# Sparse/differential attention trunk: layer 0's first projections in two contraction halves, half of its conditioning rows on TensorE

## The chip, the cores and the metric

One NeuronCore of one Trainium2 chip runs the whole program. The metric is the device time of one execution in microseconds, from the first to the last instruction and the little that lies around them. Half of a per cent is about 12 us here.

## What is computed

A decoder trunk of two layers on 256 tokens with 2048 features, in fp32. Each layer is a token mixer and a squared-ReLU MLP, and each of these four parts is conditioned by shift, scale and gate vectors that come from one vector `c`:

```python
mod_all = jnp.einsum('bd,lde->lbe', jax.nn.silu(c), ada_w) + ada_b[:, None, :]
for i in range(DEPTH):
    sh1, sc1, g1, sh2, sc2, g2 = jnp.split(mod_all[i][:, None, :], 6, axis=-1)
    h = rms_norm(x, attn_norm_g[i]) * (1.0 + sc1) + sh1
    y = nsa_mixer(h, ...) if i % 2 == 0 else diff_mixer(h, ...)
    x = x + g1 * y
    h = rms_norm(x, mlp_norm_g[i]) * (1.0 + sc2) + sh2
    x = x + g2 * sqrelu_mlp(h, mlp_w1[i], mlp_w2[i])
```

The mixer of layer 0 projects `h` to 16 query heads (`q`), and to `kc, vc, ks, vs, kw, vw` (512 columns each) and 48 gates. `kc` and `vc` are compressed: 32 tokens at a time plus a position term, through a matrix of 4096 by 256, SiLU, and a matrix of 256 by 128. Each query head then has three branches (compressed, selected, window) with their own softmax, mixed by the gates. Layer 1's mixer is differential attention.

## The kernel before

Features lie on the 128 partitions in 16 tiles (`kt`), tokens in the free dimension. Weights are read once, in pieces of 128x1024 (`load`, 512 KB each, pool of 5). Most products are made of three fp32r matmuls: `split` writes a rounded copy `wH` on ScalarE and the rest `wL` on VectorE, and `xs_mm` or `ws_mm` multiply high by high, high by low and low by high. A few products use plain fp32 matmuls without a split; each of these appears in the trace as two MATMUL records.

A conditioning element is the dot product of one row of 2048 numbers with silu(c); 128 of them (one kt of one vector) are one `ada` row, a DMA of 1 MB and one VectorE instruction with an accumulator (line 163, for the first two vectors line 170). There are 12 vectors of 16 rows. The first two are read in the opening loop; the other 160 stand in the list `ada_q`, and `ada_step(rate)` takes rows from it as the matmul loops go on: at RA, RB, RC rows per step in the first mixer. Their buffer pool has three (`adap`), and the instruction has lowered priority. The tile framework orders each engine's instructions by priority and readiness before the run; on the chip each engine and each DMA queue then runs in that order.

The stages of layer 0's mixer, in the order of the code:

- lines 639 to 654, the opening loop: for each kt two ada rows, two pieces of `ws` (1 MB), the modulated `h`, then eight fp32 matmuls of 256 columns for kc and vc (line 650) and four of 512 for vs and vw (line 654).
- lines 682 to 764: position tables (`trig`, `rope_table`), then ks and kw as split products (`xs_group` k0 and k1), each interleaved with the compression of kc or vc (`cmp_part`, 32 fp32 matmuls each with 64 stationary columns, line 705); then the gates.
- lines 768 to 834: four groups of four heads. The query projection of a group fills TensorE while the heads before it go through softmax on ScalarE and VectorE.
- `w_out_phase` (line 546): the output projection `nwo` in four blocks of 512 features; three quarters of the first two blocks are done before the last heads end. `residual` adds each block to x, and the next norm's input `z` is scaled (`Turn.ready`, `Turn.scale`): for blocks 0 to 2 in one burst after block 2 (line 534).
- `mlp`: starts with the pair of blocks `m_z`.

PSUM has eight banks: four of pool `mm`, one `sd`, three `sc`. `sd` is shared by all transposes, outputs and statistics.

Of the kernel before, what the change touches and what calls it, by code (L numbers as in the profile page):

```python
# [19 lines left out]
P = 128  # L20
# [16 lines left out]
RA, RB, RC = 1.3, 1.2, 1.6  # L37
# [19 lines left out]
WS_COLS = 4 * 512  # L57
# [18 lines left out]
def emit(ctx, tc, nc, a):  # L76
# [42 lines left out]
    posi = cst.tile([P, 3], I32, name="posi")  # L119
    xT = xp.tile([P, KT, T], F32, name="xT")  # L120
# [36 lines left out]

    def ada_tile(l, vec, kt):
# [14 lines left out]
    def ada_vec(l, vec):  # L173
        e = vec * KT
        m = mod[:, l, vec, :]
        tt(m, acc_tile(l, vec), bT[:, l, e:e + KT], ALU.add)

    ada_q = []
    for l in range(DEPTH):
        for vec in range(6):  # L180
            if (l, vec) in ((0, 0), (0, 1)):
                continue
            for kt in range(KT):
                ada_q.append((l, vec, kt))
    ada_pos = [0]
    ada_credit = [0.0]

    def ada_step(rate):
        ada_credit[0] += rate
        while ada_credit[0] >= 1.0 - 1e-9 and ada_pos[0] < len(ada_q):  # L190
            l, vec, kt = ada_q[ada_pos[0]]
            ada_tile(l, vec, kt)
            ada_pos[0] += 1
            ada_credit[0] -= 1.0
            if kt == KT - 1:
                ada_vec(l, vec)

    def ada_until(l, vec):
        while ada_pos[0] < len(ada_q) and ada_q[ada_pos[0]][:2] <= (l, vec):
            ada_credit[0] = 0.0  # L200
            ada_step(1.0)

# [203 lines left out]
    def rope_table(row, lo, n, name):  # L406
        rb = sm.tile([P, 2, HALF], F32, tag="rb", name="rb", bufs=1)
        nc.scalar.dma_start(rb.rearrange("p a b -> p (a b)"),
                            a["rows"][:, row * DH:(row + 1) * DH].to_broadcast([P, DH]))
# [62 lines left out]
    class Turn:  # L472
# [4 lines left out]
        def ready(self):  # L477
            l, w = self.l, self.which
            ada_until(l, 4 if w else 1)
            make_A(l, w)  # L480
# [43 lines left out]
    def residual(tn, ps, nb, l, vec, stats, wide=False):  # L524
        for n in range(4):
# [4 lines left out]
            if stats:  # L530
                if nb == 3 or l == 1 or vec == 5:
                    tn.scale(kt)
                tn.st.add(kt)
        if stats and nb == 2 and l == 0 and vec == 2:
            tn.ready()
            for kt in range(12):
                tn.scale(kt)
# [8 lines left out]
    def w_out_phase(name, src, tiles, l, rate, extra=None):  # L546
# [7 lines left out]
        if l == 1:  # L554
            tn.ready()
        for nb in range(4):
# [22 lines left out]
    def mlp(l, tn, rates, final):  # L579
        for c in range(4):  # L580
# [28 lines left out]
            if last:  # L609
                tn = Turn(l + 1, 0)  # L610
                tn.ready()
# [25 lines left out]
    ps_c = [[mm_tile(f"psc{i}{b}") for b in range(2)] for i in range(2)]  # L637
    ps_v = [[sc("psv00"), sc("psv01")], [sc("psv10"), sd("psv11")]]
    for kt in range(KT):
# [4 lines left out]
        wc = load(a["ws"][kt, :, :1024])  # L644
        wv = load(a["ws"][kt, :, 1024:])
        full = modulate_full(h, kt, rstd, Amod[:, 0, 0, kt:kt + 1], mod[:, 0, 0, kt:kt + 1])
        f, la = kt == 0, kt == KT - 1
        for i in range(2):
            for n in range(4):
                TE.matmul(ps_c[i][n // 2][:, (n % 2) * T:(n % 2 + 1) * T], wc[:, i * 512 + n * P:i * 512 + (n + 1) * P],  # L650
                          full, start=f and n % 2 == 0, stop=la and n % 2 == 1)
        for i in range(2):
            for t in range(TT):
                TE.matmul(ps_v[i][t], full[:, t * P:(t + 1) * P], wv[:, i * 512:(i + 1) * 512], start=f, stop=la)
    kcT = [actp.tile([P, GROUPS, 272], F32, tag="act", name=f"kcT{i}") for i in range(2)]
    for i in range(2):
        V.memset(kcT[i][:, :, 256:272], 0.0)
        for b in range(2):
            src = ps_c[i][b].rearrange("p (g t) -> p g t", g=2)
            if b:  # L660
                V.tensor_copy(kcT[i][:, 2:4, 0:T], src)
            else:
                act(kcT[i][:, 0:2, 0:T], src)
    for i in range(2):
        for t in range(TT):
            act(Vt[:, t, i, :], ps_v[i][t])

    def gates():
        H, L = split(load(a["wg"], KT * GATES), KT * GATES)
# [12 lines left out]
    nc.sync.dma_start(posi, a["posT"])  # L682
    trig()
    mk = wkp.tile([P, 288], F32, tag="qT", name="mk", bufs=1)
    nc.sync.dma_start(mk, a["consts"][:, CO_M0:CO_N])
    V.tensor_copy(maskb, mk)
    V.tensor_copy(identb, ident)
    tab_c = rope_table(ROW_KC, 2, 1, "tab_c")
    posE = smallT[:, SM_POS:SM_POS + 2 * CMP_BLOCK]
    w2c = wkp.tile([P, 2, 2, DH], F32, tag="qT", name="w2c", bufs=1)  # L690
    nc.scalar.dma_start(w2c, a["cw2"])
    def cmp_start(i):
        return sc("hidps")

    def cmp_part(i, hp, lu):
        kv = kcT[i].rearrange("p g (n l) -> p l g n", l=CMP_STRIDE)
        raws = [load(a["cw1"][i, lu, :, q * 1024:(q + 1) * 1024]) for q in range(2)]
        bl = actp.tile([P, 8, 4, 16], F32, tag="act", name="bl")
        l0 = lu * 8
        n0 = l0 // CMP_STRIDE  # L700
        tt(bl, kv[:, l0 % CMP_STRIDE:l0 % CMP_STRIDE + 8, :, n0:n0 + 16],
           posE[:, i * CMP_BLOCK + l0:i * CMP_BLOCK + l0 + 8].unsqueeze(2).unsqueeze(3)
           .to_broadcast([P, 8, 4, 16]), ALU.add)
# [4 lines left out]
    def cmp_end(i, hp):  # L708
        e = wkp.tile([64, 256], F32, tag="PcT", name="he", bufs=1)
        act(e, hp[:64, :256], AF.Exp, scale=-1.0)  # L710
        ts(e, e, 1.0, None, ALU.add)
        V.reciprocal(e, e)
        tt(e, hp[:64, :256], e, ALU.mult)
        tp = sd("htp")
        for f in range(2):
            TE.transpose(tp[:, f * 64:(f + 1) * 64], e[:, f * P:(f + 1) * P], ident[:64, :64])
        if i == 0:
            hT = wkp.tile([P, 2, 64], F32, tag="PcT", name="hT", bufs=1)
            V.tensor_copy(hT, tp[:, :128].rearrange("p (f n) -> p f n", f=2))
            kp = sd("kcp")  # L720
            for f in range(2):
                TE.matmul(kp[:64, :DH], hT[:, f, :], w2c[:, 0, f, :], start=(f == 0), stop=(f == 1))
            kr = k_norm_rope(kp[:64, :DH].unsqueeze(1), tab_c, 0, 1, 64)
            kq = sd("kcq")
            TE.transpose(kq[:, :64], kr[:64, 0, :], ident[:64, :64])
            V.tensor_copy(kT[:, :, 256:272], kq[:, :64].rearrange("p (g n) -> p g n", g=4))
        else:
            hT = wkp.tile([P, 2, 64], F32, tag="PcT", name="hTv", bufs=1)
            V.tensor_copy(hT, tp[:, :128].rearrange("p (f n) -> p f n", f=2))
            vp = sd("vcp")  # L730
            for g in range(4):
                for f in range(2):
# [340 lines left out]
```

## Time and profile before

| | |
|---|---|
| median of the runs | 2375.66 us (lowest 2375.36) |
| profiled execution | 2378.76 us, span of its instructions 2376.8 us |
| TensorE busy | 2336.5 us, 98% of the span |
| VectorE, ScalarE busy | 1753.3 us, 1178.4 us |
| granted TensorE clock, mean | 0.996 |
| read from HBM | 607.81 MB, 257 GB/s over the span |

Another run of the three took 4816.36 us; nothing here rests on it. Busy time of TensorE is the sum of its matmul records, whose ends are modelled; two records that follow each other overlap, so what a matmul costs is read from the distance between two starts. A row of the timeline gives the start, the length, the engine, the line, what is written from what, and how often; in square brackets the idle time before it and what ended it.

### The profile page before, as it was taken

To read this page: it belongs to the slowest core of one execution; us is meant where nothing else is said; L and a number is where in the kernel's file an instruction comes from. 1 tells how busy PE (TensorE), PEld (TensorE's weight loads), DVE (VectorE), ACT (ScalarE), POOL (GpSimd) and SP (SyncE) were. 2 spreads that over 40 slices of the span, in tenths; PEclk is the share of its full clock that TensorE was granted. 3 is DMA by queue.
4 is the path that set the end of the run, shared out by engine and by line. 5 is a ranking of instruction groups with operands and counts; after the bars stand their busy time and mean duration, and the time that the engine had idled before them with its cause. 6 is when DMAs were issued, how large, how long until landed. Compare 5 with 4: busy or idle time off the path is not lost.

```text
span 2376.8 us, 34755 instructions
## 1 busy us (share of the span) xinstructions
PE 2336.5 (98%) x13331; PEld 1998.2 (84%) x13331; DVE 1753.3 (74%) x2504; ACT 1178.4 (50%) x2026; POOL 43.4 (2%) x41
## 2 busy tenths in 40 slices
PE   8999999999999999999999999999999999999999
PEld 5666778999888888888888887799988888888888
DVE  6776998999888888888888776766755555555555
ACT  2123576556435435435456565554643543553553
POOL 0000000000000000000000110100000000000000
PEclk9999999999999999999999999999999999999999
DMA  9998867778888988888776667546565555565564
GB/s 369 420 352 308 314 236 286 290 286 335 332 316 315 328 324 316 309 332 316 297 277 220 224 222 247 187 152 191 176 191 186 186 187 186 186 187 187 186 196 149
DMA packets 141718, 612.18 MB, mean 258 GB/s; under 512 B 15856, under 2 KB 17264, under 8 KB 116976
## 3 DMA queue, kind: packets, MB, share of 16 engines
q1 hardware_dynamic: 140400, 609.05, 72.1%
q8 instruction: 104, 1.70, 0.3%
q10 hardware_dynamic: 1152, 0.92, 0.2%
q14 instruction: 62, 0.51, 0.1%
HBM read 607.81 MB, written 2.10 MB: 257 GB/s over the span
## 4 chain that ended last, share of the span: by engine, by line
PE 69%; DVE 2%; DMA 1%; issue 1%; ACT 1%; POOL 1%; SPq 0%; DVEq 0%; POOLq 0%
PE m L239 36%; PE m L246 17%; PE dwo L232 1%; PE dwo L231 1%; PE dwo L233 1%; PE m L242 1%; DMA adaraw<-adaT 1%; PE dk L223 1%; PE dk L224 1%; PE dk L225 1%; DVE wL L98 1%; PE m_z L232 1%; PE m_z L233 1%; PE m_z L231 1%; PE dv L224 1%
## 5 line engine op out<-in xcount | busy, mean ns | idle before, releaser
L95 ACT ACTIVATE wH<-raw 128x1024 fp32r<-128x1024 f32 x721 | 762.2, 1059 | 889.4 <-PE m L239 666.3
L98 DVE TENSOR_TENSOR wL<-raw,wH 128x1024 fp32r<-128x1024 f32 x721 | 876.9, 1221 | 429.7 <-ACT wH L95 428.5
L239 PE MATMUL m<-hd,wH 128*128 128x512 f32 x2048 | 712.3, 396 | 0.0
L239 PE MATMUL m<-hn,wH 128*128 128x512 f32 x1792 | 625.3, 397 | 0.0
L246 PE MATMUL m<-hd,wL 128*128 128x256 f32 x1920 | 537.1, 281 | 3.4 <-DVE wL L98 3.4
L246 PE MATMUL m<-hn,wL 128*128 128x256 f32 x1680 | 471.5, 281 | 0.0
L239 PEld LDWEIGHTS m<-hd,wH 128*128 128x128 f32 x2048 | 376.9, 188 | 81.0
L239 PEld LDWEIGHTS m<-hn,wH 128*128 128x128 f32 x1792 | 329.9, 188 | 70.8
L101 DVE SCALAR_TENSOR_TENSOR adaraw<-adaraw,cbc 128x2048 f32<-128x2048 f32 x160 | 365.3, 2284 | 23.6 <-DMA adaraw<-adaT 23.3
L246 PEld LDWEIGHTS m<-hd,wL 128*128 128x128 f32 x1920 | 361.7, 189 | 10.7 <-DVE wL L98 4.6
L246 PEld LDWEIGHTS m<-hn,wL 128*128 128x128 f32 x1680 | 317.8, 189 | 5.6 <-DVE wL L98 0.2
L101 DVE SCALAR_TENSOR_TENSOR xT<-m,mod,xT 128x256 f32<-128x256 f32 x256 | 108.5, 477 | 38.4 <-PE m L239 38.3
L101 DVE SCALAR_TENSOR_TENSOR adarow<-adarow,cbc 128x2048 f32<-128x2048 f32 x32 | 73.2, 2287 | 13.2 <-DMA adarow<-adaT 10.3
L233 PE MATMUL nwo<-o,wL 128*128 128x256 f32 x256 | 73.4, 288 | 2.4 <-DVE wL L98 2.4
L232 PE MATMUL nwo<-o,wH 128*128 128x256 f32 x256 | 74.0, 289 | 0.0
L231 PE MATMUL nwo<-o,wH 128*128 128x256 f32 x256 | 73.7, 288 | 0.0
L231 PE MATMUL dwo<-od,wH 128*128 128x256 f32 x256 | 72.9, 285 | 0.0
L231 PE MATMUL m_z<-z,wH 128*128 128x258 f32 x256 | 72.3, 284 | 0.0
L232 PE MATMUL dwo<-od,wH 128*128 128x256 f32 x256 | 72.2, 282 | 0.0
L232 PE MATMUL m_z<-z,wH 128*128 128x258 f32 x256 | 72.1, 283 | 0.0
L233 PE MATMUL dwo<-od,wL 128*128 128x256 f32 x256 | 72.1, 282 | 0.0
L233 PE MATMUL m_z<-z,wL 128*128 128x258 f32 x256 | 71.5, 283 | 0.5 <-DVE wL L98 0.5
(300 smaller groups left out, 3216.6 us busy)
## 6 DMA issues: line engine op xcount, KB each, us to landing
raw<-w SPq DMA_DIRECT2D x512, 512.0 KB, 4.4
adaraw<-adaT SPq DMA_DIRECT2D x160, 1024.0 KB, 7.2
raw<-di SPq DMA_DIRECT2D x96, 512.0 KB, 4.2
adarow<-adaT SPq DMA_DIRECT2D x32, 1024.0 KB, 11.8
raw<-wi SPq DMA_DIRECT2D x48, 512.0 KB, 5.7
raw<-ws SPq DMA_DIRECT2D x32, 512.0 KB, 10.0
raw<-nwo SPq DMA_DIRECT2D x32, 512.0 KB, 5.6
raw<-dwo SPq DMA_DIRECT2D x32, 512.0 KB, 3.5
```

Of the source, the lines that this page charges most:

```text
L95: return S.activation(out=out, in_=in_, func=func, **kw)
L98: V.tensor_tensor(out=out, in0=in0, in1=in1, op=op)
L101: V.scalar_tensor_tensor(out, in0, scalar, in1, op0=op0, op1=op1, **kw)
L223: TE.matmul(ps, xh, H[:, off:off + n], start=first, stop=False)
L224: TE.matmul(ps, xh, L[:, off:off + n], start=False, stop=False)
L225: TE.matmul(ps, xl, H[:, off:off + n], start=False, stop=last)
L231: TE.matmul(ps, H[:, off:off + m], xh, start=first, stop=False)
L232: TE.matmul(ps, H[:, off:off + m], xl, start=False, stop=False)
L233: TE.matmul(ps, L[:, off:off + m], xh, start=False, stop=last)
L239: big = lambda stop: TE.matmul(ps.rearrange("p (a t) -> p a t", a=2), H[:, off:off + P], at, start=first, stop=stop)
L242: TE.matmul(ps[:, :T], L[:, off:off + P], at[:, 0], start=False, stop=False)
L246: TE.matmul(ps[:, :T], L[:, off:off + P], at[:, 0], start=False, stop=False)
```

## The change

The opening loop becomes four loops (HK is 8): kc, vc, vs, vw for kt 0 to 7 in plain fp32; ks and kw for kt 0 to 7 as split products, with two pairs of ada rows of later kts in between; kc, vc (fp32) and ks, kw (now fp32) for kt 8 to 15, the ada rows read two kts ahead; vs and vw for kt 8 to 15 as split products, with the compression in its last five steps. The halves of vs and vw are added on VectorE. The position tables are computed in the first loop. In the compression the matmuls for kc and vc alternate and write to two halves of PSUM's partitions from two groups of 64 columns of the array; the position term is added where kc and vc leave PSUM.

Rows of layer 0's vectors 3 and 4 that stand at place 24 or later in the list (24 of them; the order of vectors is now 2, 4, 3, 5) go to TensorE. Each is 16 fp32 matmuls with a 32-column stationary operand (silu(c) repeated) and a moving operand of 128 columns, in turn to four column groups, whose sums stand on four groups of 32 partitions; ScalarE copies the result, one more fp32 matmul adds the four groups, and ScalarE adds the bias. In the heads some small VectorE instructions are merged or go to ScalarE. `ready` is split: scale factors before the output projection's last parts, shifts before its last block; `scale` then follows each residual.

```diff
-RA, RB, RC = 1.3, 1.2, 1.6
+RA, RB, RC = 1.0, 1.25, 1.5
+PE_FROM = 24
+PE_LAG = 2
...
+    def on_pe(l, vec, kt):
+        return l == 0 and vec in (3, 4) and ada_q.index((l, vec, kt)) >= PE_FROM
+
+    def pe_row(l, vec, kt, r):
+        w = r.rearrange("p (k n) -> p k n", k=KT)
+        ps = sd("aps")
+        for k in range(KT):
+            i = k % 4
+            TE.matmul(ps[i * 32:(i + 1) * 32, :P], cs[:, k:k + 1].to_broadcast([P, 32]), w[:, k], start=k < 4, stop=k >= KT - 4,
+                      tile_position=(0, i * 32))
+        four = sm.tile([P, P], F32, tag="jk", name="four", bufs=1)
+        act(four, ps[:, :P])
+        TE.matmul(ps[:, P:P + 1], four, e4, start=True, stop=True)
+        e = vec * KT + kt
+        act(mod[:, l, vec, kt:kt + 1], ps[:, P:P + 1], AF.Identity, bias=bT[:, l, e:e + 1])
...
+        if on_pe(l, vec, kt):
+            pe_rows.append((l, vec, kt, r))
+            pe_flush(PE_LAG)
+            return
...
-        if l == 1:
-            tn.ready()
+        tn.ready_scale()
         for nb in range(4):
...
+            if nb == 3:
+                tn.ready_shift()
             residual(tn, ps, nb, l, 2, True)
...
+    for kt in range(HK):
+        lead_ada(kt)
+        wc = wcols(kt, 0)
+        wv = wcols(kt, 1)
+        full = full_of(kt)
+        c_mm(wc, full, kt == 0, False)
+        row_mm(ps_v, wv, full, kt == 0, kt == HK - 1)
...
+    for kt in range(HK):
+        H, L = split(wcols(kt, 2))
+        for i in range(2):
+            for t in range(TT):
+                xs_mm(ps_k[i][t], h, kt, t, H, L, i * 512, 512, kt == 0, False)
+        if kt in (2, 5):
+            lead_ada(HK + kt // 3)
+
+    for kt in range(HK, KT):
+        if kt + 2 < KT:
+            lead_ada(kt + 2)
+        wc = wcols(kt, 0)
+        wk = wcols(kt, 2)
+        full = full_of(kt)
+        c_mm(wc, full, False, kt == KT - 1)
+        row_mm(ps_k, wk, full, False, kt == KT - 1)
...
         for j in range(8):
-            TE.matmul(hp[:64, :256], bl[:, j].rearrange("p g n -> p (g n)"),
-                      raws[j // 4][:, j % 4 * 256:(j % 4 + 1) * 256], start=(l0 + j == 0), stop=(l0 + j == 31))
+            for i in range(2):
+                x = kcT[i][:, z].rearrange("p g (n l) -> p l g n", l=CMP_STRIDE)[:, l0 + j]
+                w = wk[:, j] if i == 0 else wv[j // 4][:, j % 4 * 256:(j % 4 + 1) * 256]
+                TE.matmul(hp[i * 64:(i + 1) * 64, :256], x, w, start=(lu + j == 0), stop=(lu * 8 + j == 31),
+                          tile_position=(0, i * 64))
...
+    for kt in range(HK, KT):
+        H, L = ahead.pop(0) if ahead else split(wcols(kt, 1))
+        for i in range(2):
+            for t in range(TT):
+                xs_mm(ps_w[i][t], h, kt, t, H, L, i * 512, 512, kt == HK, kt == KT - 1)
...
+            cmp_part(hp, lu)
+        if kt - HK >= 4:
+            ada_step(RA)
...
+    for i in range(2):
+        for t in range(TT):
+            tt(Vt[:, t, i, :], ps_w[i][t], Vt[:, t, i, :], ALU.add)
...
-                ts(mx, mx, qss[t][:, 1, r:r + 1], None, ALU.mult)
+                act(mx, mx, AF.Copy, scale=qss[t][:, 1, r:r + 1])
```

## Rows read from the trace of the kernel before

**Rows 1.** The page: busy time of TensorE and VectorE; chain that ended last

```profile
PE 2336.5 (98%) x13331; PEld 1998.2 (84%) x13331; DVE 1753.3 (74%) x2504; ACT 1178.4 (50%) x2026; POOL 43.4 (2%) x41
PE 69%; DVE 2%; DMA 1%; issue 1%; ACT 1%; POOL 1%; SPq 0%; DVEq 0%; POOLq 0%
```

**Rows 2.** Busy time by stage: opening loop's halves, k stage, heads, output projection

```profile
core 0: us, PE busy (x) PEld busy (x) DVE busy (x) ACT busy (x) POOL busy (x), PEclk, DMA share, GB/s
24.20:83.50 59.30, 58.26 (x192) 38.07 (x192) 45.79 (x64) 7.03 (x16) 0.00 (x0) 0.95 1.00 399
83.50:144.40 60.90, 56.19 (x194) 35.87 (x193) 46.69 (x75) 11.50 (x23) 0.00 (x0) 1.00 0.99 399
144.40:230.60 86.20, 81.33 (x337) 55.64 (x335) 60.87 (x87) 29.63 (x69) 4.00 (x4) 0.96 0.85 317
237.50:380.80 143.30, 141.61 (x711) 109.72 (x710) 131.86 (x289) 96.35 (x273) 6.04 (x6) 1.00 0.76 281
380.80:507.90 127.10, 124.29 (x953) 117.97 (x952) 117.11 (x229) 76.68 (x188) 2.01 (x2) 0.99 0.76 286
```

**Rows 3.** Timeline of TensorE in the opening loop

```profile
33.91 3.62 PE L650 MATMUL psc<-h,raw 128*128 128x256 f32 x16
37.36 3.60 PE L654 MATMUL psv<-raw,h 128*128 128x512 f32 x8
40.79 3.62 PE L650 MATMUL psc<-h,raw 128*128 128x256 f32 x16
...
83.85 3.72 PE L650 MATMUL psc<-h,raw 128*128 128x256 f32 x16 [0.24 <-ACT h L95]
...
117.36 3.60 PE L654 MATMUL psv<-raw,h 128*128 128x512 f32 x8
123.59 3.72 PE L650 MATMUL psc<-h,raw 128*128 128x256 f32 x16 [2.63 <-ACT h L95]
...
144.38 0.79 PE L223 MATMUL k<-wH,h 128*128 128x512 f32 x1
```

**Rows 4.** The opening loop's ada rows on VectorE: ns min/median/max

```profile
L101 DVE SCALAR_TENSOR_TENSOR adarow<-adarow,cbc x32: 2281/2285/2294, 14.1 to 134.6; 128x2048 f32<-128x2048 f32 x32
```

**Rows 5.** Timeline of TensorE: two of thirteen split-product matmuls of k0

```profile
146.02 0.40 PE L224 MATMUL k<-wL,h 128*128 128x512 f32 x1
...
148.81 0.40 PE L224 MATMUL k<-wL,h 128*128 128x512 f32 x1
```

**Rows 6.** Timeline of the k stage: compression matmuls, then a wait

```profile
180.77 2.75 PE L705 MATMUL hidps<-raw,bl 128*64 128x256 f32 x12
...
185.69 0.30 PE L467 MATMUL tps<-co,krn 128*128 128x128 f32 x1 [2.17 <-DVE krn L98]
```

**Rows 7.** Stretches at half clock (PEclk), columns as in Rows 2

```profile
186.80:193.60 6.80, 6.00 (x15) 4.66 (x15) 6.62 (x12) 4.32 (x9) 0.00 (x0) 0.50 0.76 287
490.60:494.00 3.40, 3.40 (x18) 3.40 (x18) 3.40 (x4) 0.71 (x1) 0.00 (x0) 0.50 0.74 169
```

**Rows 8.** Timeline: fp32 matmuls with 16 stationary and 128 moving columns

```profile
253.11 1.92 PE L733 MATMUL vcp<-w2c,hTv 128*16 128x128 f32 x16
```

**Rows 9.** One tile by stretch: VectorE's ada rows in the output projection

```profile
380.80:507.90 127.10, 46.10 (x41) 0.99 0.76 286
```

**Rows 10.** Timeline of the output projection: VectorE's burst, then TensorE's longest wait

```profile
484.37 4.04 DVE L101 SCALAR_TENSOR_TENSOR z<-xT,Amod,z 128x256 fp32r<-128x256 f32 x10
...
489.60 0.39 PE L233 MATMUL nwo<-o,wL 128*128 128x256 f32 x1 [2.04 <-DVE wL L98]
```

**Rows 11.** Groups by shape, 237.5 to 507.9 us: small VectorE work of the heads

```profile
L804 DVE TENSOR_REDUCE mx<-sc 128x1 f32<-128x128 f32 x32 | 7.9, 282 | 1.5 <-PE sc L791 1.5
L105 DVE TENSOR_SCALAR mx<-mx,qs 128x3 f32<-128x3 f32 x32 | 6.9, 215 | 0.1
L809 DVE RECIPROCAL su<-su 128x3 f32<-128x3 f32 x32 | 5.5, 171 | 3.8 <-ACT Pm L95 3.7
```

**Rows 12.** Timeline of VectorE: work on the position tables

```profile
148.94 1.16 DVE L101 SCALAR_TENSOR_TENSOR trb<-trb 128x192 f32<-128x192 f32 x3
```

More of the change, by code (lines that the diff above doesn't have):

```diff
@@ L196, in ada_step @@
                 ada_vec(l, vec)
+                ada_have.add((l, vec))
     def ada_until(l, vec):
-        while ada_pos[0] < len(ada_q) and ada_q[ada_pos[0]][:2] <= (l, vec):
+        while (l, vec) not in ada_have:
             ada_credit[0] = 0.0
             ada_step(1.0)
+        if any(p[:2] == (l, vec) for p in pe_rows):
+            pe_flush()
     def split(raw, n=1024):
@@ L530, in residual @@
             if stats:
-                if nb == 3 or l == 1 or vec == 5:
-                    tn.scale(kt)
+                tn.scale(kt)
                 tn.st.add(kt)
-        if stats and nb == 2 and l == 0 and vec == 2:
-            tn.ready()
-            for kt in range(12):
-                tn.scale(kt)
     pend = []
@@ L655, in emit @@
[L655 to L663, printed above, removed]
+                TE.matmul(ps[i][t], full[:, t * P:(t + 1) * P], w[:, i * 512:(i + 1) * 512], start=f, stop=la)
@@ L664, in emit @@
     for i in range(2):
         for t in range(TT):
-            act(Vt[:, t, i, :], ps_v[i][t])
-    def gates():
-        H, L = split(load(a["wg"], KT * GATES), KT * GATES)
+            if t:
+                V.tensor_copy(Vt[:, t, i, :], ps_v[i][t])
+            else:
+                act(Vt[:, t, i, :], ps_v[i][t])
+    ps_k = four("psk")
+    for kt in range(HK):
[5 more added lines that the diff above has]
+            lead_ada(HK + kt // 3)
@@ new lines, in emit @@
+    for kt in range(HK, KT):
[6 more added lines that the diff above has]
+        row_mm(ps_k, wk, full, False, kt == KT - 1)
+    posE = smallT[:, SM_POS:SM_POS + 2 * CMP_BLOCK]
+    kcT = [actp.tile([P, 2, GROUPS, T], F32, tag="act", name=f"kcT{i}") for i in range(2)]
+    ahead = [split(wcols(HK + q, 1)) for q in range(2)]
+    for i in range(2):
+        V.memset(kcT[i][:, 1, :, T - CMP_STRIDE:], 0.0)
+        for b in range(2):
+            src = ps_c[i][b].rearrange("p (g n l) -> p g n l", g=2, l=CMP_STRIDE)
+            for z in range(2):
+                pos = posE[:, i * CMP_BLOCK + z * CMP_STRIDE:i * CMP_BLOCK + (z + 1) * CMP_STRIDE]
+                nb = T // CMP_STRIDE - z
+                dst = kcT[i][:, z, b * 2:b * 2 + 2].rearrange("p g (n l) -> p g n l", l=CMP_STRIDE)
+                tt(dst[:, :, :nb], src[:, :, z:],
+                   pos.unsqueeze(1).unsqueeze(1).to_broadcast([P, 2, nb, CMP_STRIDE]), ALU.add)
@@ L738, in emit, with cmp_keys @@
-    tab_ks = rope_table(ROW_KS, 0, 2, "tab_ks")
-    tab_kw = rope_table(ROW_KW, 0, 2, "tab_kw")
+            TE.transpose(tp[:, f * P:(f + 1) * P], e[:, f * P:(f + 1) * P], ident)
+        ct["h"] = wkp.tile([P, 2, P], F32, tag="PcT", name="hT", bufs=1)
+        act(ct["h"], tp[:, :256].rearrange("p (f n) -> p f n", f=2))
+    def cmp_keys():
+        kp = sd("kcp")
+        for f in range(2):
+            TE.matmul(kp[:64, :DH], ct["h"][:, f, :64], w2c[:, 0, f, :], start=(f == 0), stop=(f == 1))
+        ct["k"] = k_norm_rope(kp[:64, :DH].unsqueeze(1), tab_c, 0, 1, 64)
@@ new lines, in cmp_values @@
+    def cmp_values():
+        vp = sd("vcp")
+        for g in range(4):
+            for f in range(2):
+                TE.matmul(vp[:16, g * DH:(g + 1) * DH], ct["h"][:, f, 64 + g * 16:64 + (g + 1) * 16], w2c[:, 1, f, :],
+                          start=(f == 0), stop=(f == 1))
+        ts(vcmp[:16].rearrange("p g d -> p (g d)"), vp[:16, :], rowmask, None, ALU.mult)
+        kq = sd("kcq")
+        TE.transpose(kq[:, :64], ct["k"][:64, 0, :], ident[:64, :64])
+        V.tensor_copy(kT[:, :, 256:272], kq[:, :64].rearrange("p (g n) -> p g n", g=4))
```

184 lines of the change are left out of this document (93 added, 91 removed).

## The prediction

> **What bounds the kernel now.** I read the page first. TensorE is busy 98% of the span and carries 69% of the chain that ended last; VectorE is busy 74% [rows 1]. Busy time of TensorE says little by itself, so the second view is the busy time by stage. In the opening loop the DMA engines are busy all the time (share 1.00 and 0.99), and VectorE 46 of 60 us. In the heads and the output projection the DMA share is 0.76, and VectorE is busy 131.9 of 143.3 and 117.1 of 127.1 us [rows 2]. The reader is to see two kinds of stage: one in which weights can be late, and two in which VectorE has little air. After these stages the change touches only the order of a few rows.
>
> Third, the timelines, for the distance between starts, which is what a matmul costs. One kt of the opening loop takes 40.79 - 33.91 = 6.88 us when nothing waits: 3.45 for kc and vc, 3.43 for vs and vw [rows 3]. A split product costs (148.81 - 146.02)/12 = 0.2325 us per matmul [rows 5], so 12 of them, which are one kt of two 512-column blocks, 2.79 us. The compression issues 12 records in 2.75 us, 0.22 each without the tail of the last [rows 6]; its 128 records are 28 us.
>
> With these prices the lost time can be read off. From 83.85 to 144.38 us the loop's second half takes 60.5 us for 8 x 6.88 = 55.0, so 5.5 are lost; the longest wait ends at 123.59, where the 3.60 us of records that began at 117.36 were long over [rows 3]. The k stage takes 86.2 us [rows 2] for 16 x 2.79 + 28 = 72.6 and some 2 of transposes: 11 to 12 are lost, among them a wait of 2.17 us for `krn` [rows 6] and 6.8 us at half clock [rows 7], half of which is loss. In the output projection one wait of 2.04 us for `wL` stands behind a burst of ten `z` instructions on VectorE [rows 10], and 3.4 us at half clock follow [rows 7]. So VectorE's load costs TensorE here about 2.0 + 1.7 us that can be named, not the 10 us by which the engine's busy time falls short of the stage or the 46.1 us that ada rows hold VectorE [rows 9].
>
> **Projections.** The work on TensorE does not change: before 16 x 6.88 + 16 x 2.79, after twice 8 x 6.88 and twice 8 x 2.79, 154.7 us in both. What changes is what stands beside it. The 32 ada rows (32 MB) are spread over 24 steps instead of 16, and the second fp32 half has its rows two steps ahead and none in its last two steps: of 5.5 us lost I take 4 back (bounds 0 and 5.5). The key norms get the whole fourth loop, so the wait for `krn` and the half clock behind it go: of 11.6 us I take 5 (bounds 0 and 11.6).
>
> New costs in this part: the tables move into the first loop, nineteen instructions of at most 1.16/3 = 0.39 us [rows 12], some 7 us, and the table DMAs pass the weights on SP's queue there. VectorE has 59.3 - 45.8 = 13.5 us free in that half [rows 2], but the DMAs have none; 3 us. kc and vc now leave PSUM by eight VectorE instructions instead of two engines' copies, and the four `mm` banks are wanted at once by vs and vw: the last kt's row matmuls (3.43 us) cover about half, 2 us. The fourth loop has splits, two key norms, the PSUM copies and four ada rows on VectorE, nearly all of the old stage's 60.9 us [rows 2], beside 8 x 2.79 + 14 to 28 of TensorE: 3 us. Together 8 (bounds 0 and 15).
>
> **Compression.** 64 pairs of matmuls, each to its own half of the array's columns. Nothing in this trace runs two matmuls side by side. If pairs overlap, 14 us go; if not, nothing. I take 14, because the two have different columns, weights and PSUM partitions.
>
> **Rows on TensorE.** 24 rows leave VectorE, 24 x 2.285 = 55 us there [rows 4]. On TensorE a row is 16 fp32 matmuls, 32 records, with 128 moving columns. The nearest row is `vcp`: 16 records in 1.92 us, 0.12 each, although only 16 columns are stationary [rows 8]; a narrow operand alone saves nothing. One after another a row costs 32 x 0.12 = 3.84 us, at four abreast 0.96, plus 0.24 for the two records that add the groups. 24 rows cost 29 us at 1.2, at least 23 if the adding hides, and 98 at 4.08. I take 29, for the reason given for pairs, and keep 98.
>
> The page "TensorE: Matmul & The Clock Gate" of the Trainium skill, Part 3, gives a measured gain of 2.38 for three column groups at 512 columns; by that share four give 3.2, a row 1.45 us and 24 rows 35, an estimate that no run here shows yet.
>
> All 24 rows fall into the output projection: RA and RB issue 4 + 20 rows before it, RC 9 by the early parts and 15 in the rest. There VectorE's relief gives back the named 2.0 + 1.7 us, say 4 (bounds 0 and 8). This is the heart of the forecast: TensorE, the bound, takes on 29 us to give back 4.
>
> **Heads.** One maximum merged (at most 0.28 us), one scaling less on two tiles (2 x 0.22), one reciprocal less (0.17) for each of 16 heads [rows 11]: 14 us of VectorE in 143. The stage's TensorE waits are short; 3 us (bounds 0 and 6). The ScalarE instructions added (two small ones per head) are hidden, since it is busy 96 of 143 us [rows 2]; without that cover they would cost the same again.
>
> **After it.** Seven fewer rows are done when the MLP begins (48, where before RA, RB and RC gave 55), so vector 5 is completed by a burst of four rows, 9 us of VectorE, beside a block of the MLP whose PSUM has a second side. The shifts are finished just before `m_z`, behind the last three rows. 2 us together (bounds 0 and 6).
>
> **Sum,** against the profiled span: 2376.8 - 4 - 5 + 8 - 14 - 3 - 4 + 29 + 2 = 2385.8. The execution lies 2.0 above its span and the median of the runs 3.1 below the execution, so 2384.7; I say 2385, no change by a 2% measure (47.5 us).
>
> **Rivals.**
>
> *The column groups run one after another,* so the change doesn't do what it says: rows cost 98 instead of 29, the compression saves nothing: 2385 + 69 + 14 = 2468, slower. For it: no two records of this trace share the array, and `vcp` is not cheaper for 16 columns. Against it: four sums are kept apart by column and partition. With the pairs overlapping, a row decides for slower from (47.5 + 20)/24 = 2.8 us. The same page, Part 3, says that weights load during a running matmul only when the row groups differ, and here all groups use all rows; by that rule this rival holds. The trace agrees only in part: in [rows 5] matmuls on all rows with new weights each time start every 0.23 us though each lasts 0.40.
>
> *The array empties at each change of arrangement.* Two changes per row and eight in the compression, each losing the overlap of neighbours, 0.40 - 0.23 = 0.17 us [rows 5]: 56 x 0.17 = 9.5, so 2394. The page "TensorEngine Tiling (Array Packing)", Key Properties, states that changing the tiling mode drains the engine; no run here shows it.
>
> *TensorE waits in its own queue.* A row's matmuls need its DMA, and the adding needs ScalarE's copy; behind either stand all `nwo` matmuls, and the row's buffer also holds the next row's DMA on SP's queue. Two rows of lag and the order worked out beforehand speak against it; one `wL` wait of 2.04 us in this stage [rows 10] shows what a miss costs. At 1.2 us per row 29 us, 2414.
>
> *All recoveries at their bounds:* -5.5 - 11.6 - 14 - 6 - 8 + 23 = -22, 2354. Faster by over 2% it would be only if TensorE lost work that none of these rows shows.
>
> **How the numbers follow.** Forecast (2365 to 2405) 0.50; draining 0.13; queue waits 0.12; serial groups 0.14; the low bounds 0.11. The range reaches from 2354 to 2430: it leaves out the serial case and half of the lowest. Faster by over 2% (about what a measurement of this kernel can tell from no change) 0.02, slower 0.14 and a little of the waits, 0.16, within 0.82. The likeliest own range is 2365 to 2405.
>
> **What would show it.** In the profile after: the heads begin at about 222 instead of 237.5 us; the fp32 second half keeps 6.9 us per kt; the compression's two matmuls of a pair start almost together and the stage's 128 records take 14 us; the output projection lasts 127 - 4 + 29 = 152 us, with VectorE below 75% there; a row's 32 records span about 1 us. If a row spans over 3 us, the serial rival is right; if gaps stand before the adding matmul, the queue waits. The forecast is wrong if the output projection stays near 127 us, or if the opening stages grow.

## The result and the profile after

The changed kernel takes 2399.61 us (median of four runs, 2397.46 to 2404.51) against 2375.66 us of the kernel before in the same comparison (median of three): ratio 1.010, 95% interval 1.0083 to 1.0117. It is slower by 24 us where 9 were forecast, within 2%. One execution in four of the kernel before (4816 us), one in ten of opening_alone and one in four of half_rows were far longer than the others and are left out of the medians given here. The profiled execution took 2399.87 us, its span is 2397.6.

The page, the lines that answer to [rows 1] (busy time of the engines; the chain that ended last):

```profile
PE 2356.7 (98%) x14145; PEld 2021.4 (84%) x14145; DVE 1693.5 (71%) x2375; ACT 1193.8 (50%) x2102; POOL 40.7 (2%) x41
PE 88%; DVE 5%; DMA 4%; ACT 1%; issue 1%; POOL 1%; SPq 0%; DVEq 0%; POOLq 0%; ACTq 0%
```

VectorE lost 60 us of work and TensorE gained 20. Busy time by stage, columns as in [rows 2]: the opening up to the first query matmul, the query groups with the heads, the output projection, the pair `m_z`, and the first blocks of the MLP's second matrix:

```profile
23.00:213.00 190.00, 182.93 (x760) 128.93 (x761) 140.79 (x215) 48.34 (x106) 5.74 (x4) 0.98 0.96 378
213.00:373.30 160.30, 154.75 (x780) 121.17 (x778) 129.37 (x259) 115.04 (x342) 7.50 (x7) 0.98 0.66 249
373.30:521.10 147.80, 146.54 (x1637) 132.96 (x1635) 69.65 (x137) 77.59 (x199) 2.01 (x2) 1.00 0.66 247
521.10:572.20 51.10, 51.10 (x467) 50.11 (x464) 42.15 (x73) 31.90 (x60) 0.00 (x0) 1.00 0.72 248
617.40:719.40 102.00, 93.03 (x513) 80.26 (x512) 86.94 (x98) 37.24 (x39) 0.00 (x0) 0.95 0.87 329
```

Before, the same boundaries lay at 237.5, 380.8, 507.9, 556.4 and 601.5 to 693.9 us. So the first query matmul comes 24.5 us earlier; the stretch from there to the MLP, which I call the middle from here on, takes 308.1 instead of 270.4 (+37.7); `m_z` takes 2.6 more; the block of the last line takes 9.6 more (102.0 for 92.4). The rest of the kernel is 4.6 us shorter; 3.5 of that is idle time of TensorE after the last block (7.9 for 11.4 us), which was not followed further. Together +20.8, the difference of the spans.

Not all 24 rows stand in the middle. Of their 768 records 704, that is 22 rows, fall into the output projection, and two rows fall into `m_z`, whose 2.6 us are about their price. The tile of the rows alone, TensorE's busy time first:

```profile
373.30:521.10 147.80, 25.74 (x704) 18.26 (x704) 0.00 (x0) 1.00 0.66 247
```

The rows on TensorE, in its timeline, one row with its adding matmuls (L180) and the `nwo` matmuls around it:

```profile
470.30 0.28 PE L268 MATMUL nwo<-o,wH 128*128 128x256 f32 x1
470.51 1.08 PE L176 MATMUL aps<-adaraw,cs 128*32 128x128 f32 x32
471.52 0.38 PE L269 MATMUL nwo<-o,wH 128*128 128x256 f32 x1
...
471.98 0.28 PE L269 MATMUL nwo<-o,wH 128*128 128x256 f32 x1
472.10 0.28 PE L180 MATMUL aps<-e,four 128*128 128x1 f32 x2
472.24 0.36 PE L270 MATMUL nwo<-o,wL 128*128 128x256 f32 x1
472.44 0.28 PE L268 MATMUL nwo<-o,wH 128*128 128x256 f32 x1
```

32 records take 1.01 us from start to start, where `vcp` would make it 3.84 [rows 8]; before them the next start comes after 0.21 us instead of 0.12, and the adding takes 0.14 and delays the next by 0.08. An undisturbed row costs some 1.3 us. The compression's pairs, in the same timeline:

```profile
174.35 0.38 PE L785 MATMUL hidps<-cwk,kcT 128*64 128x256 f32 x1
174.35 0.38 PE L785 MATMUL hidps<-raw,kcT 128*64 128x256 f32 x1
174.56 0.38 PE L785 MATMUL hidps<-cwk,kcT 128*64 128x256 f32 x1
174.57 0.38 PE L785 MATMUL hidps<-raw,kcT 128*64 128x256 f32 x1
```

Two start together and the next two 0.21 us later, what one record took before [rows 6].

The block of the last line of the stages. First the queue SP; then ScalarE and TensorE, with the idle time before each and what ended it; then half clock, columns as in [rows 7]:

```profile
622.14 16.45 SPq L191 DMA_DIRECT2D adaraw<-adaT  x5
638.68 1.84 SPq L250 DMA_DIRECT2D raw<-w  x4
```

```profile
645.34 1.06 ACT L98 ACTIVATE wH<-raw 128x1024 fp32r<-128x1024 f32 x1 [12.78 <-DMA raw<-w]
646.45 2.08 PE L276 MATMUL m<-hd,wH 128*128 128x512 f32 x4 [6.41 <-ACT wH L98]
651.08 1.23 PE L283 MATMUL m<-hd,wL 128*128 128x256 f32 x4 [2.56 <-DVE wL L101]
```

```profile
644.50:654.60 10.10, 5.59 (x16) 4.29 (x17) 9.95 (x15) 3.17 (x3) 0.00 (x0) 0.50 0.97 378
```

Five row DMAs stand on SP for 16.45 us, most of it until VectorE gives one of three buffers back; the weights come behind them. ScalarE waits 12.78 us for such weights and TensorE 6.41 us for ScalarE's rounded copy of them. Another 2.56 us TensorE waits for `wL` from VectorE, which has five rows and eight residuals to do first. These are its 9 idle us in that block (102.0 - 93.03), and it goes on at half clock.

**An account of the middle.** Of each run I take the length of the middle, subtract TensorE's idle time (length less busy time in the two lines of its stages) and the loss at half clock (length times what PEclk lacks to 1). What is left is TensorE's own work:

| kernel | middle | idle | half-clock loss | left |
|---|---|---|---|---|
| before | 270.4 | 4.5 | 1.3 | 264.6 |
| after | 308.1 | 6.8 | 3.2 | 298.1 |
| rows_on_vector | 282.7 | 14.0 | 5.3 | 263.4 |
| rows_vector_rates | 286.4 | 14.7 | 8.4 | 263.3 |
| opening_alone | 290.2 | 15.2 | 10.2 | 264.8 |
| opening_heads | 280.6 | 12.0 | 6.9 | 261.7 |
| half_rows | 283.6 | 11.0 | 6.9 | 265.7 |
| ra_more | 284.5 | 14.3 | 4.4 | 265.8 |
| eight_rows | 281.2 | 4.2 | 3.1 | 273.9 |
| rc_two | 333.1 | 20.1 | 13.6 | 299.4 |
| lag_one | 332.7 | 19.2 | 10.1 | 303.4 |

Each line is one execution, and the executions of one kernel differ by 2 to 13 us. The last column is good to 2 or 3 us: PEclk has two places, and time that TensorE idles at half clock is subtracted twice. It is 262 to 266 us with no rows on TensorE, 274 with eight (seven of them in the middle), 298 for the changed kernel with 22 there, 299 and 303 with all 24. So a row costs 1.3 to 1.6 us, and nothing else changes TensorE's work by more than that error. All the rest of the differences is waiting. The experiments ask what TensorE waits for.

### The profile page after: what moved, and what is told of

The parts are those of the page before. It is cut to its first block, busy times and chain, and to the rows that moved or that the text cites. A ratio compares the mean times of both kernels' runs of the same rounds, so it can differ in the third digit from the quotient of the medians.

```text
span 2397.6 us, 36317 instructions
## 1 busy us (share of the span) xinstructions
PE 2356.7 (98%) x14145; PEld 2021.4 (84%) x14145; DVE 1693.5 (71%) x2375; ACT 1193.8 (50%) x2102; POOL 40.7 (2%) x41
## 4 chain that ended last, share of the span: by engine, by line
PE 88%; DVE 5%; DMA 4%; ACT 1%; issue 1%; POOL 1%; SPq 0%; DVEq 0%; POOLq 0%; ACTq 0%
PE m L276 37%; PE m L283 17%; DMA adaraw<-adaT 2%; PE psc L689 1%; PE nwo L268 1%; PE nwo L270 1%; PE m_z L270 1%; PE m_z L268 1%; PE dwo L269 1%; PE m_z L269 1%; PE nwo L269 1%; PE dwo L270 1%; PE dwo L268 1%; DVE wL L101 1%; PE m L279 1%
## 5 line engine op out<-in xcount | busy, mean ns | idle before, releaser
L104 DVE SCALAR_TENSOR_TENSOR adaraw<-adaraw,cbc 128x2048 f32<-128x2048 f32 x136 | 310.7, 2286 | 39.3 <-DMA adaraw<-adaT 39.3
```

The costliest lines, as they stand in the source:

```text
L104: V.scalar_tensor_tensor(out, in0, scalar, in1, op0=op0, op1=op1, **kw)
```

## Experiments

### Rows and column groups

**rows_on_vector**

```diff
-PE_FROM = 24
+PE_FROM = 48
```

> The changed kernel with all ada rows of layer 0 on VectorE again (no row from place 24 on goes to TensorE; order of the vectors, rates and everything else as changed). Theory: the 24 rows hold TensorE, the bound, 24.3 + 4.3 us in the stretch 373 to 521 and a little after it, some 31 us, and relieve nothing that TensorE waited for, so without them the stretch from the first query matmul to the MLP shrinks from 308 to about 278 us and the time from 2399.6 to about 2370 (2362 to 2376). Rival: VectorE needed the relief; with 24 x 2.29 = 55 us more it is busy 125 of the output projection's some 120 us, TensorE waits for wL and the stretch stays near 300 us: 2388 to 2400.

Measured: 2379.47 us, ratio to before 1.0007 (0.9997 to 1.0017). Between the two. The rows on TensorE cost 20.1 us net: the account of the middle gives 34.7 for the work of 22 of them, and 9 us less waiting in return. Both theories were half right; TensorE carries the rows' whole price, and VectorE's relief is worth more than nothing.

**one_group**

```diff
-            i = k % 4
-            TE.matmul(ps[i * 32:(i + 1) * 32, :P], ..., start=k < 4, stop=k >= KT - 4, tile_position=(0, i * 32))
+            TE.matmul(ps[:32, :P], ..., start=k == 0, stop=k == KT - 1, tile_position=(0, 0))
...
-        TE.matmul(ps[:, P:P + 1], four, e4, start=True, stop=True)
+        TE.matmul(ps[:, P:P + 1], four[:32], e4[:32], start=True, stop=True)
```

> The changed kernel with the 16 matmuls of a row all sent to the first group of 32 columns, one after another, instead of four groups in turn; the adding matmul then reads one group of 32 partitions. Theory: the groups run abreast (in the changed kernel's trace four starts lie within 0.03 us), so a row goes from about 1.2 to 32 x 0.11 + 0.2 = 3.7 us: 24 x 2.5 = 60 us more, 2460 (2445 to 2475). Rival: the starts say little and the array serves the groups one after another anyway: 2396 to 2404.

Measured: 2465.4 us, 65.8 more than the changed kernel, 2.7 per row. A row's 32 records here:

```profile
488.94 3.68 PE L175 MATMUL aps<-adaraw,cs 128*32 128x128 f32 x32
```

The four column groups do run abreast; the first rival of the prediction is out, and its price of 98 us for 24 rows in a line would have been nearly right (1.3 + 2.7 = 4.0 each).

**eight_rows**

```diff
-RA, RB, RC = 1.0, 1.25, 1.5
-PE_FROM = 24
+RA, RB, RC = 1.0, 1.6, 1.6
+PE_FROM = 40
```

> The changed kernel with rows from place 40 on (8 instead of 24) on TensorE, and RB and RC 1.6 as in rows_vector_rates (2369.3), which has none there. Theory: VectorE and TensorE share the bound of the output projection; eight rows take 19 us from VectorE and put 10 on TensorE, so the stretch gets a little shorter: 2362 (2357 to 2367). Rival: each row on TensorE costs its price and gives nothing back, 8 x 1.3 = 10 us more, with waits behind its chain: 2378 to 2384.

Measured: 2368.42 us (ratio 0.9968, 0.9954 to 0.9982), against 2369.28 for rows_vector_rates, no difference. In the account the middle's waits shrink (idle 14.7 to 4.2 us, half clock 8.4 to 3.1) and TensorE takes 10.6 more: the middle gains 5 us, and `m_z` (5 us longer) and the first blocks behind it (2) give them back. Neither expected range was met. Eight rows pay for themselves, 24 don't.

### The burst at the MLP's start

**vec5_earlier**

```diff
-CR = (0, 0, 1, 1, 1)
+CR = (0, 0, 1, 2, 1)
```

> The changed kernel with rate 2 instead of 1 in the MLP's fourth block of the first chunk, so that the 64 rows of layer 0 are all issued before the second matrix's first block ends and no burst of four follows it. Theory: the burst puts five row DMAs one behind the other on SP's queue, each waiting for one of three buffers, for 16 us; the weights behind them come late, TensorE idles 6.4 us and runs 10.2 us at half clock. Without the burst the stretch 617 to 719 falls from 102 to 92 us and the time from 2399.6 to about 2389 (2386 to 2392). Rival: VectorE, not the queue, is late there (eight residuals and splits behind four rows); moving four rows one block earlier only moves the wait: 2396 to 2402.

Measured: 2403.15 us, no gain; the rival's number and a little more. The block after the burst takes 94.6 instead of 102.0 us, but the one before it 51.2 instead of 45.2:

```profile
578.70:629.90 51.20, 45.84 (x259) 39.06 (x257) 47.66 (x53) 28.29 (x47) 0.00 (x0) 0.98 0.93 370
629.90:724.50 94.60, 92.84 (x512) 79.97 (x513) 79.22 (x88) 35.25 (x34) 0.00 (x0) 0.97 0.87 330
```

The wait moved with the rows; there is no room for them on either side of that point. Whether the queue or VectorE is late there this run does not tell apart. In the changed kernel it is both, 6.41 us by the queue and 2.56 by VectorE, as the lines above show.

**rows_vector_vec5**

```diff
-PE_FROM = 24
-CR = (0, 0, 1, 1, 1)
+PE_FROM = 48
+CR = (0, 0, 1, 2, 1)
```

> Both edits: all rows on VectorE and rate 2 in that block. Theory: the two losses are independent and add, 2399.6 - 30 - 11 = about 2359 (2351 to 2366), which would beat the kernel before by the opening stages' 24 us less some 6. Rival (VectorE needed the relief): 2378 to 2392.

Measured: 2380.0 us, as rows_on_vector without the second edit; the rival. The second edit is worth nothing here either.

**rows_vector_rates**

```diff
-RA, RB, RC = 1.0, 1.25, 1.5
-PE_FROM = 24
+RA, RB, RC = 1.0, 1.6, 1.6
+PE_FROM = 48
```

> The kernel of rows_on_vector (all rows on VectorE, the rest as changed) with RB and RC 1.6, which gives the same counts as the kernel before (29.6 and 55). Theory as for rc_two: the loss at the MLP's start goes and 2379.5 becomes 2369 (2364 to 2373). Rival: VectorE has no room in the heads and the output projection for seven rows more, 16 us: 2376 to 2384.

Measured: 2369.28 us (ratio 0.9967, 0.9954 to 0.9981), as the theory had it, 10.2 less than rows_on_vector. The block that took 102.7 us there:

```profile
596.00:686.10 90.10, 90.10 (x513) 78.49 (x512) 76.43 (x88) 37.25 (x39) 0.00 (x0) 1.00 0.87 324
```

The middle pays 3.7 us for the seven rows, the MLP's start gains 12.6. So the loss there is the price of the changed kernel's RB and RC, which put seven rows off, and done earlier on VectorE the rows cost a third of it.

**rc_two**

```diff
-RA, RB, RC = 1.0, 1.25, 1.5
+RA, RB, RC = 1.0, 1.25, 2.0
```

> The changed kernel with RC 2.0 instead of 1.5: 56 instead of 48 rows are issued when the MLP begins, as in the kernel before (55). Rows 24 to 47 stay on TensorE. Theory: the 10 us that the MLP's start lost (147 us for the blocks after m_z, 137.5 before) are the price of seven rows put off from the output projection, where the DMA engines are busy 0.66, into blocks where they are busy 0.97; done earlier they cost nothing: 2389 (2385 to 2393). Rival: the output projection has no room either, since its rows on TensorE now come closer together: 2396 to 2404.

Measured: 2413.7 us, 14 more than the changed kernel; the rival, and beyond it. The MLP's block does take 90.1 us, but the output projection 173.6 instead of 147.8. Waits in it (in total, times, longest), first in the changed kernel, then here:

```profile
SPq L191 <- PE aps L176: 88.4, 21, 8.1
ACT wH L98 <- DMA raw<-nwo: 4.7, 2, 4.2
```

```profile
SPq L191 <- PE aps L176: 88.4, 24, 10.2
ACT wH L98 <- DMA raw<-nwo: 16.1, 6, 5.2
PE aps L180 <- ACT four L98: 4.5, 10, 0.6
```

The row DMAs stand on SP for buffers that TensorE holds, but they do so just as long in the changed kernel, where TensorE idles 1.3 us in this stage. What is new here is that ScalarE waits 16.1 us for weights of `nwo` instead of 4.7, and that TensorE stands before its own rows. Of its 15.1 idle us, 4.5 are spent before the adding matmul, for ScalarE's copy, and 2.5 before a next row, until ScalarE has read the PSUM bank; each of these is 0.4 in the changed kernel. What sets off what is not shown.

**lag_one**

```diff
-PE_LAG = 2
+PE_LAG = 1
```

> The kernel of rc_two (2413.7) with PE_LAG 1 instead of 2, so that one row instead of two waits with its buffer before TensorE takes it. Theory: in rc_two SP's queue stands 88 us for row buffers that TensorE holds, the output projection's weights stand behind these DMAs, and TensorE idles 15 us and runs 20 us at half clock; a buffer given back one row sooner takes most of that away: 2394 to 2402. Rival: the waits come from the row's own chain (copy on ScalarE, one PSUM bank for all rows); with less lag the row's DMA is late for its matmuls on top: 2412 or more.

Here the edit is to rc_two. Measured: 2409.67 us, a gain of 4 where the theory had 12 to 20. Idle time and half clock fall by 4 of 34 us; SP still waits for TensorE's rows 84 us in place of 88, which says little, since the changed kernel has the 88 too. So how long a row's buffer is kept is at most a small part of it. Whether one PSUM bank for all rows, the copy on ScalarE or the three buffers themselves make rc_two's waits stays open; a fourth buffer was not tried.

### Where the opening's gain goes

**opening_alone** (relative to the changed kernel: rows, order of vectors, heads, `ready` and the burst of `z` as before the change)

```diff
-RA, RB, RC = 1.0, 1.25, 1.5
-PE_FROM = 24
+RA, RB, RC = 1.0, 1.6, 1.6
+PE_FROM = 48
...
-        for vec in ((2, 4, 3, 5) if l == 0 else range(6)):
+        for vec in ((2, 3, 4, 5) if l == 0 else range(6)):
...
+        if stats and nb == 2 and l == 0 and vec == 2:
+            tn.ready()
+            for kt in range(12):
+                tn.scale(kt)
...
-                act(mx, mx, AF.Copy, scale=qss[t][:, 1, r:r + 1])
+                ts(mx, mx, qss[t][:, 1, r:r + 1], None, ALU.mult)
```

> One part of the change alone: the four opening loops with the compression in column pairs, all else as in the kernel before (heads, output projection with one burst of z after block 2, vectors in the order 2 3 4 5, all rows on VectorE); RB 1.6 so that as many rows are done before the output projection (29.6) and before the MLP (55) as in the kernel before. Theory: the opening's gain, some 22 us at the first query matmul (215 instead of 237.5), is kept whole, and nothing later moves: 2355 (2349 to 2362). Rival: the query groups and the output projection have got slower because the opening hands its VectorE and DMA work on to them, so that the stretch from the first query matmul to the MLP is 280 us here too: 2365 to 2375.

Measured: 2375.32 us, ratio 0.9999 (0.9990 to 1.0009). The rival, and a little more: the first query matmul comes at 214.6 us, 22.9 earlier, and nothing of it is left. By the account the middle is 19.8 us longer than before, and its waits alone are 19.6 us longer. The middle, by its two stages:

```profile
214.60:359.20 144.60, 140.06 (x680) 107.67 (x679) 134.86 (x272) 88.76 (x252) 6.59 (x7) 0.98 0.80 305
359.20:504.80 145.60, 134.99 (x989) 125.15 (x989) 132.98 (x265) 85.35 (x212) 2.02 (x2) 0.95 0.76 286
```

VectorE is busy 267.8 of 290.2 us, 92%, the share that it had before (131.9 + 117.1 of 270.4 [rows 2]), with 18.9 us more to do. The extra work is ada rows, which hold VectorE 116.0 us in the middle instead of 96.2. Most of them come from the stage ahead: the old k stage held VectorE 23.0 us with them, the new opening holds it 9.2. One line of each, the tile of the rows alone (VectorE's busy time and its instructions), before and in this kernel:

```profile
144.40:237.50 93.10, 23.04 (x21) 0.96 0.86 318
```

```profile
22.00:214.60 192.60, 9.18 (x8) 0.97 0.95 373
```

And the heads end late. The last head's output matmul starts at 445.9 us, where it started at 445.5 before, although the heads had a head start of 23 us. First and last starts before, here, and in the next two kernels:

```profile
L832 PE MATMUL ops<-PT,vcmp x32: 379/380/382, 286.4 to 445.5; 128*128 128x256 f32 x32
L924 PE MATMUL ops<-PT,vcmp x32: 379/382/634, 267.3 to 445.9; 128*128 128x256 f32 x32
```

**opening_heads** (opening_alone with the heads as changed)

```diff
-                ts(mx, mx, qss[t][:, 1, r:r + 1], None, ALU.mult)
+                act(mx, mx, AF.Copy, scale=qss[t][:, 1, r:r + 1])
```

and the merged maximum, reciprocal and product of the change.

> The kernel of opening_alone with the merged small instructions of the heads as well. Theory: the heads end earlier, so the wait for the query norms is no longer covered by other matmuls; nothing is gained and 3 to 6 us are lost: 2358 to 2361. Rival: the 14 us less on VectorE shorten the heads' stretch: 2348 to 2352.

Measured: 2365.3 us (ratio 0.9955, 0.9940 to 0.9970), the fastest of the kernels that do the whole work, 10.0 less than opening_alone. My theory was wrong in sign; both ranges were missed, since they stood on 2355 for opening_alone. The last head comes at 422.3:

```profile
L929 PE MATMUL ops<-PT,vcmp x32: 379/380/382, 268.3 to 422.3; 128*128 128x256 f32 x32
```

Of the 12 us that TensorE still idles in the middle, one wait makes up 7.39. It stands behind residuals and the burst of ten `z` instructions on VectorE, where a wait of 2.04 us stood before [rows 10]:

```profile
466.91 4.04 DVE L104 SCALAR_TENSOR_TENSOR z<-xT,Amod,z 128x256 fp32r<-128x256 f32 x10
472.15 0.58 PE L270 MATMUL nwo<-o,wL 128*128 128x256 f32 x1 [7.39 <-DVE wL L101]
```

**half_rows** (opening_alone with the later rows of layer 0 at half length: half of each dot product is left out)

```diff
-            stt(r, r, 1.0, cbc, ALU.mult, ALU.mult, accum_out=acc_tile(l, vec)[:, kt:kt + 1])
+            n = D // 2 if l == 0 else D
+            stt(r[:, :n], r[:, :n], 1.0, cbc[:, :n], ALU.mult, ALU.mult, accum_out=acc_tile(l, vec)[:, kt:kt + 1])
```

> The kernel of opening_alone whose 64 later rows of layer 0 are multiplied over 1024 instead of 2048 elements (half of each dot product of layer 0's vectors 2 to 5 is left out); their DMAs stay whole, TensorE's work is the same. Theory: from the first query matmul to the MLP VectorE sets the pace, not TensorE (it is busy 92% of that stretch in the kernel before, 249 of 270 us, and 92% with the opening alone, 268 of 290), and the opening's 22 us are eaten there because 14 us of ada rows that VectorE did in the old k stage now fall into it. With 51 rows at half price, 58 us less on VectorE, the stretch falls from 290 to 265 to 270 us and the time from 2375.8 to about 2353 (2346 to 2360). Rival: late weights or the row DMAs on SP's queue set the pace there; then halving VectorE's part changes little: 2370 to 2377.

Measured: 2362.01 us (ratio 0.9945, 0.9926 to 0.9965), 13.3 less than opening_alone: a little over half of what the theory had, and not the rival. The heads end at 414.8; the middle's two stages stand below:

```profile
L925 PE MATMUL ops<-PT,vcmp x32: 379/380/382, 267.0 to 414.8; 128*128 128x256 f32 x32
```

```profile
215.80:372.40 156.60, 152.19 (x765) 119.02 (x764) 124.86 (x333) 107.13 (x314) 6.59 (x7) 0.98 0.77 294
372.40:499.40 127.00, 120.42 (x911) 113.71 (x909) 97.86 (x213) 69.38 (x158) 2.01 (x2) 0.97 0.81 314
```

VectorE is now busy 222.7 of 283.6 us, 26 less than in the middle before the change (249.0), and the waits are still 18 us in the account, 12 more than before. So VectorE's load is part of what eats the opening's gain: the middle shortens by 6.6 of the 19.8 us that it had grown, and most of what else is gained comes in `m_z` (46.6 for 50.4 us). The other waits stay when VectorE is relieved: single waits for `wH` and `wL` and 6.9 us of loss at half clock. I don't know why the earlier start brings these.

**ra_more** (opening_heads with the rows put back into the opening)

```diff
-RA, RB, RC = 1.0, 1.6, 1.6
+RA, RB, RC = 2.6, 1.2, 1.6
```

> The kernel of opening_heads (2365.3) with RA 2.6 and RB 1.2 instead of 1.0 and 1.6: ten rows in the last opening loop as in the old k stage, fewer in the heads, the same count before the output projection. Theory: the opening's gain and VectorE's six rows are one account; the rows fit into that loop only where its DMAs let them (share 0.91 already), so the first query matmul comes some 8 us later, the stretch after it is some 10 us shorter, and the sum is 2360 to 2366. Rival: the fourth loop has free time on VectorE (32 of 51 us busy), the rows cost nothing there and the stretch gains all of 15 us: 2349 to 2354.

Measured: 2374.0 us, 8.7 more than opening_heads, outside both expectations. VectorE's rows in the opening are 22.8 us again; the first query matmul comes at 220.2, 4 us later, and the middle takes 284.5, 4 us more instead of 10 less. Fewer rows in the heads did not shorten them. VectorE is busy 250.9 us in the middle, as much as before the change (249.0), and the waits there are 18.7 us, where they were 5.8:

```profile
220.20:379.70 159.50, 153.11 (x761) 119.25 (x762) 134.84 (x261) 113.43 (x336) 8.57 (x7) 0.98 0.68 261
379.70:504.70 125.00, 117.07 (x905) 111.72 (x904) 116.05 (x190) 70.21 (x163) 2.01 (x2) 0.99 0.83 319
```

So the rows that moved out of the opening do not, by themselves, account for the lost gain. The idea of opening and middle as one account, one for one, falls.

## Why the prediction was right or wrong

The direction and the range held; the size did not (24 us for 9). That the time still lies in the likeliest range is in part luck: the opening gained 9.5 us more than forecast, while the rows, the heads and the burst all cost more. The terms of the sum, in its order:

| term | forecast | measured |
|---|---|---|
| opening: second half, waits, new costs, compression | -4 -5 +8 -14 = -15 | -24.5 |
| rows on TensorE | +29 | +36.1 (33.5 in the middle, 298.1 - 264.6, and 2.6 in `m_z`) |
| heads, waits given back | -3 | +7.1 (waits 1.7 to 8.8) |
| output projection, waits given back | -4 | -2.8 (waits 4.1 to 1.3) |
| the burst | +2 | +9.6 |
| the rest | 0 | -4.6 |
| sum | +9 | +20.8 (rounded terms) |

**Rows.** The step that split "one after another" from "four abreast" by the row of `vcp` was right, and one_group shows both prices. A row came out at 1.5 instead of 1.2 us by the account of the middle (33.5 for 22 rows; the forecast put all 24 there). By the starts of an undisturbed row it is 1.3, and the difference to 1.2 is what the starts before and behind a row lose; the other 0.2 us are not located. This loss is the draining of the second rival, with half of its price: 0.2 us per row, 5 in all, an estimate from the starts shown above. The trace of the kernel before already held it, which the prediction overlooked: from the last `k` matmul to the first compression matmul with 64 stationary columns it is 0.33 us (150.44 to 150.77) instead of 0.2325 [rows 5]. Where the Trainium skill ("TensorEngine Tiling (Array Packing)", Key Properties) lets the engine drain at a change of mode, the starts around a row agree, by 0.1 to 0.2 us. Another rule of the Trainium skill, that weights load under a running matmul only for other row groups ("TensorE: Matmul & The Clock Gate", Part 3), does not hold here: the pairs that start together share all rows, and the weights of the pair at 174.35 us load from 174.12 on, while the pair before runs from 174.03 to 174.51.

**Opening.** The recoveries came much as forecast, and the new costs of 8 us were too high. The fp32 second half takes 56.4 us for 60.9 before (4.5 back, 4 forecast). The first half takes 60.3 for 59.3, so the tables cost 1 us and not 3. The old k stage with the gates took 93.1 us, and the two loops in its place take 22.7 and 50.6. That is 19.8 less: the 14 us of the compression, as the pairs' starts say, and 5.8 where 5 back and 5 of new costs were forecast. A little of the gain is only moved: the compression's key matmuls (`kcp`) now start at 226 us, behind the first query matmul, and before at 210, ahead of it. And the first matmul of the loops comes 1.2 us earlier. The forecast's 222 us for the first query matmul was 213.

**Heads and output projection.** I read [rows 9, 10] as VectorE costing TensorE 3.7 us, and priced its relief at that. For the output projection this came out nearly right: its waits fell by 2.8 us. In the heads the argument failed. I took their waits for short [rows 2] and priced only their decrease, as if they did not depend on when TensorE comes to the heads. They rose by 7.1 us in the changed kernel, although VectorE is busy there 129.4 of 160.3 us where it was 131.9 of 143.3. Of the 5.6 us idle, 5.0 stand before transposes and scores, for the heads' own instructions on VectorE and ScalarE:

```profile
PE tps L502 <- DVE qr L101: 2.3, 3, 1.2
PE tps L502 <- DVE mx L899: 2.0, 2, 1.7
PE sc L882 <- ACT qT L98: 0.7, 1, 0.7
```

opening_alone shows the same in full: the opening's gain is all lost in waits. The step that failed is that the stages behind the opening keep their waits when it gets shorter. What makes the waits is only in part shown. VectorE's load is a part of it: less of it gained 10.0 us in opening_heads and 13.3 in half_rows. That the 14 us of rows which the shorter opening no longer holds are the cause, as opening_alone suggests, is not shown: ra_more puts them back and loses 8.7, which speaks against it. The rest stays open.

What the change does about VectorE is worth more than I gave it: the heads' small instructions 10.0 us, measured beside the opening alone (forecast 3, bound 6), the rows on TensorE some 9 us of waits (forecast 4, bound 8). But the rows cost 34.7 in the middle to give back 9, which was the heart of the forecast, and it held.

**The burst.** I saw the seven rows put off and the burst of four, and covered it by VectorE's 9 us and the second PSUM side: 2 us, at most 6. It costs 9.6, and 12.6 are gained at that place in rows_vector_rates. The failed step is that I priced VectorE's part and not the queue's: the row DMAs wait on SP for buffers, the weights stand behind them (6.41 of the 9 idle us; VectorE's own part is 2.56), and TensorE goes on at half clock for some 10 us. I had named this very mechanism, for the output projection. There, in the changed kernel, the row DMAs do stand on SP for 88 us, but TensorE idles only 1.3.

**Rivals.** Serial groups: out. Draining: true in part, 5 us. Queue waits: not where I put them, but true at the MLP's start; in rc_two, TensorE does stand before the adding and late weights, with the cause open. All recoveries at their bounds: out; the opening came nearest, with 24.5 of at most 31.

The best kernel of the study is opening_heads: the four opening loops, the compression in pairs and the leaner heads, with all rows on VectorE and rates that keep the counts of before: 2365.3 us, 0.45% faster than before and 1.4% faster than the changed kernel. Its lead of 3 us on eight_rows and 4 on rows_vector_rates is no more than the executions of these kernels differ.

## What to carry to other kernels

When a stage gets shorter, ask what the stages behind it will then wait for: a gain of 23 us at one point of the timeline was worth nothing at the end, and 10 to 13 us of it came back when VectorE's load behind it was cut. Work moved onto the engine that is the bound is paid in full, and what it relieves gives back only the waits that can be counted. A DMA that must wait for a buffer stands in the same queue as the weights behind it, so a rate of side loads has to be priced by the queue, not only by the engine that uses them up. What such a wait costs depends on how soon those weights are needed: 16 us on SP cost TensorE 6.4 us at the MLP's start, 88 us in the output projection next to nothing.

## What the runs showed of the hardware

fp32 matmuls on separate column groups do run side by side. Two groups of 64 columns: two records per 0.21 us. Four groups of 32 columns: 32 records with 128 moving columns in 1.01 us, where all on one group cost 2.7 us more per row. Each change between this arrangement and the ordinary one lost about 0.1 us between starts; so did the change from 128 to 64 stationary columns in the kernel before, where nothing ran side by side.
